# Hymba-style block in fp32 on one core: part of the depthwise convolution's taps as adding transfers, the layer norm dealt earlier

## Chip, core and metric

The kernel runs on one core of a Trainium2 chip. The metric is the device time of one execution in microseconds (us). The version before took 2039.97 us, the median of three runs (2035.58 to 2040.53).

## The reference, cut to what matters

The input x has 256 rows of 4096 columns, in float32. All weights are float32 and are read once from DRAM; w_in alone has 4096 x 14336 elements.

```python
xn = rms_norm(h, norm_in_g[i])
proj = xn @ w_in[i]
q, k, v, z_a, a_c, g_c, z_c = jnp.split(
    proj, np.cumsum([ATT_WIDTH] * 4 + [CONV_WIDTH] * 2)[:6].tolist(), axis=-1)
...
y_a = rms_norm(y_a, attn_out_g[i]) * jax.nn.silu(z_a)
y_c = conv_module(a_c, g_c, w_dw[i], b_dw[i], conv_ln_g[i], conv_ln_b[i], w_pw[i], b_pw[i])
y_c = rms_norm(y_c, conv_out_g[i]) * jax.nn.silu(z_c)
h = h + jnp.concatenate([y_a, y_c], axis=-1) @ w_out[i]
gate = jax.nn.sigmoid(rms_norm(h, ple_norm_g[i]) @ w_ple_gate[i] + b_ple_gate[i])
h = h + gate * (p[i] @ w_ple[i])
```

The change concerns conv_module: u = a * sigmoid(g), then for each of 2048 channels a causal filter of 31 taps over the 256 rows (u shifted by 30 - k rows, times w_dw[k], summed over k), plus a bias; then a layer norm over the channels, silu, and the product with w_pw. y_a is chunked attention with 16 heads of 128 and a relative bias.

## The kernel before, in words

**Products.** A product of 256 rows with 4096 x 1024 weights goes over 16 pairs of row blocks (`mixed_product`, one loop turn per pair, called a *step* here). A step loads two tiles of 512 KB with SyncE (SP) from a pool of five buffers. Each tile is split (`parts_of`): ScalarE casts it to float32r (`wh`, L218), VectorE subtracts that from the tile (`wl`, L219), and PE multiplies three times (high x high, low x high, high x low). A tile of a plain step thus costs 12 matmuls of 128x128 by 512 columns, and a plain step 24. A step called *seven* uses seven sums of blocks in place of eight products: 21 matmuls, with VectorE making the sums of weights (`ua`, `ub`, L442 to L447). There are three buffers each for wh and wl.

**The order of the products** is written out by hand: `glu_conv` 0 and 1 (columns of a and g), keys 0 (Q0 and K0), values (V0 and V1), then `attention(0)`, `glu_conv` 2 and 3, keys 1, `attention(1)`, keys 2, the layer norm's list, Q3/V2, `attention(2)`, K3/V3, `attention(3)`, then the product with w_pw, the gates z, w_out and w_ple_gate. Where a product ends, `scaled_pair` scales it by the row norm (L510), and `to_heads` transposes it (L851) and copies it (L856).

**Deferred work.** What has to be done between the steps is kept in the list `later`; after each step `deal` takes from it as many items as the product's `fills` say (`early_fills` for most products here), and one step of an attention from `heads`. Its instructions are issued behind the last cast, so the engines meet them in that place of their program. Between K3/V3 and w_pw the rest of the list is emptied in one go (`fill(len(later))`).

**The convolution.** `glu_conv(c)` makes u for 512 channels (four blocks of 128 channels, `uT`, channels on the partitions) and appends 4 x 31 taps to the list. A tap (`conv_tap`, L696) is one VectorE instruction on one block, `cv += uT shifted * w_dw[k]`, 226 to 256 columns wide. There are 16 blocks and so 16 x 30 such instructions, and 16 that start a sum.

**The layer norm** (`layer_norm_swish`) is a list too: sums over the blocks, mean by a matmul with a constant (`mean_w`), 16 centerings (L766), squares (L770) and their sums (L774), variance, then per block a multiplication and a silu on ScalarE (`swish`, L804), and a split into two float32r parts (`split`, ScalarE L814, VectorE L815), which is the stationary operand of w_pw. Empty items (`rest`) keep steps that wait for PE apart.

**Attention** (`attention(g)`, four heads) is five items in `heads`. The scores of two heads (L868, L869) get scale and bias on VectorE (L875) and their maximum (L879), ScalarE takes the exponential (L880); in the next item the weights are transposed and copied by VectorE (`pT`, L893), then multiplied by V. The bias comes by a transfer (`load_bias`), and one corner of it is overwritten by POOL (L939), which otherwise does almost nothing.

Of the kernel before, what the change touches and what calls it, by code (L numbers as in the profile page):

```python
# [21 lines left out]
NEG = -1e30  # L22
# [3 lines left out]
def hybrid_block(  # L26
# [157 lines left out]
    def behind_casts():  # L184
        return tc.issue_after(last_cast[0].ins) if last_cast else nullcontext()

    def fill(n):
        with behind_casts():
            for _ in range(min(n, len(later))):
                later.popleft()()  # L190

    heads = deque()
# [150 lines left out]
    def mixed_product(  # L343
# [67 lines left out]
        for n, (pair, seven) in enumerate(order):  # L411
            if n < done:
                continue
            if ahead:
                ahead(pair)
            wts = []
            for k in range(2):
                wt = wpool.tile([P, 2, NB], F32, tag="w", name="wt")
                nc.sync.dma_start(wt, two_columns(w, 2 * pair + k, col, apart))
                wts.append(wt)  # L420
            if n >= len(order) - n_left:
                for k in range(2):
                    tiles = left[2 * (n - len(order) + n_left) + k]
                    held.append((2 * pair + k, parts_of(wts[k], 2, tiles and tiles())[0]))
                deal(fills[n % len(fills)])
                continue
            if not seven:
                for k in range(2):
                    add_plain(n, k, *parts_of(wts[k], 2)[0])
                deal(fills[n % len(fills)])  # L430
                continue
            begins = not helper
            if begins:
                for name in ("P1", "P5", "P7", "P6"):
# [24 lines left out]
            add("P2", block(k1, 0), (w1h[:, 0], w1l[:, 0]), n, True)  # L459
            add("P3", s_of(3), (w1h[:, 1], w1l[:, 1]), n, True)  # L460
            add("P6", s_of(2), (ubh[:, 0], ubl[:, 0]), n, True)
            add("P4", block(k1, 1), (ubh[:, 1], ubl[:, 1]), n, True)
            if begins and on_begin:
                on_begin()
            if begins:
                tc.add_manual_dep(
                    made[first].ins, last_transpose[0].ins.name,
                    mybir.DependencyInfo(mybir.DependencyClass.NoSync, mybir.DependencyReason.DATA),
                    reason="transposes before the helpers take their banks",
                )  # L470
            if n == last_seven:
                on_helpers(helper)
            deal(fills[n % len(fills)])
        after.close()
        return (c, add_left) if left else c

# [210 lines left out]

    conv = []

    def conv_tap(cv, uT, i, b, k):  # L690
        if k == PAD:
            nc.vector.tensor_scalar(
                cv[:, i, :], uT[:, i, :], dw[:, b, k : k + 1], bdw[:, b : b + 1], ALU.mult, ALU.add
            )
        else:
            nc.vector.scalar_tensor_tensor(  # L696
                cv[:, i, PAD - k :], uT[:, i, : T + k - PAD], dw[:, b, k : k + 1],
                cv[:, i, PAD - k :], ALU.mult, ALU.add,
            )

    def glu_conv(c):
# [24 lines left out]
                uT[:, 2 * pair : 2 * pair + 2, :], pt.rearrange("q (i t) -> q i t", t=T)  # L726
            )
        cv = act.tile([P, 4, T], F32, tag="act", name="cv")
        for i in range(4):
            for k in reversed(range(TAPS)):  # L730
                later.append(partial(conv_tap, cv, uT, i, 4 * c + i, k))
        conv.append(cv)


    uS = []

    def layer_norm_swish():

# [76 lines left out]
            nc.vector.tensor_tensor(lo, conv[c][:, i, :], hi.bitcast(F32), ALU.subtract)  # L815

        n = len(conv)
        rest = [lambda: None] * 4
        later.extend(partial(total, c) for c in range(n))
        later.append(lambda: fold(st["s"]))  # L820
        later.extend(rest)
        later.append(lambda: mean(st["s"][:, 0, :]))
        later.extend(rest)
        for c in range(n):
            later.extend(partial(center, c, i) for i in range(4))
            later.append(partial(square, c))
        later.append(lambda: fold(st["q"]))
        later.extend(rest)
        later.append(lambda: variance(st["q"][:, 0, :]))
        later.extend(rest)  # L830
        later.append(lambda: diagonals(st["s"][:, 0, :]))
        later.extend(rest)
        later.append(lambda: spread(st["s"][:, 0, :]))
        later.extend(rest)
        for c in range(n):
            later.extend(partial(swish, c, i) for i in range(4))
        for c in range(n):
            later.extend(partial(split, c, i) for i in range(4))


    y_a = []
# [18 lines left out]

    def attention(g):
        qT, kT, v, bias = qs[g], ks.pop(g), vs.pop(g), biases.pop(g)
        y = qT.rearrange("q g (h d) -> q h g d", h=NH)
        held = {}

# [62 lines left out]
    def load_bias(g):  # L928
# [7 lines left out]
                ap=[[1, P], [span, GH], [1, T]],  # L936
            ),
        )
        nc.gpsimd.memset(bias[: P // 2, :, : P // 2], NEG)  # L939

    def queries(g, q):
        qs[g] = act.tile([P, GH, T], F32, tag="act", name="qT")
# [17 lines left out]
    def late_pool():  # L960
        nonlocal more
        first_sums.close()
        more = pool("more", 4)
        load_bias(3)

    n_g = H // GH
    assert n_g == CW // NB == 4
# [9 lines left out]
    keys(1, early_fills)  # L977
    attention(1)
    keys(2, early_fills)
    layer_norm_swish()  # L980
    load_bias(2)
    q, vs[2] = blocks((o_q + 3 * NB, o_v + 2 * NB), early, (4,))
    queries(3, q)
    attention(2)
    k, vs[3] = blocks(
        (o_k + 3 * NB, o_v + 3 * NB), valued, (5, 5, 4, 5, 4, 2, 3, 2, 3, 2, 3, 4, 4, 4, 4, 4),
        then=late_pool,
    )
    keyed(3, k)
# [8 lines left out]
        )  # L998
        return t

    fill(len(later))

    point = units("0 1 2 3 4 5 6 7")
    y_c = []
# [321 lines left out]
```

## Time and profile before

| what | before |
|---|---|
| median of three runs | 2039.97 us |
| the profiled execution | 2035.71 us |
| its span | 2033.9 us |
| PE busy | 2015.2 us, 99% |
| VectorE (DVE) busy | 1912.3 us, 94% |
| ScalarE (ACT) busy | 1184.6 us, 58% |
| GpSimd (POOL) busy | 7.7 us |
| moved by DMA | 412.28 MB, 203 GB/s on average |

The shares are of the span. A busy time counts overlapping instructions once; matmuls are pipelined, so a busy PE may still lose time between two starts. In rows of the timeline the first number is the start in us from the span's beginning, the second how long the group of instructions lasts; a bracket at the end holds the idle time of the engine ahead of it and what released it.

### The profile page before, as it was taken

What the parts mean: (1) busy time and instruction counts of PE and PEld (TensorE: products, weight loads), DVE (VectorE), ACT (ScalarE), POOL (GpSimd) and SP (SyncE); (2) the same over time, 40 slices, a digit from 0 to 9 for tenths busy, and PEclk for the clock granted to TensorE, in tenths of its full rate; (3) what the DMA queues carried; (4) which work ended last, traced back from release to release, by engine and by line L of the source; (5) the groups of instructions that cost most, each with busy time, mean ns of one, the idle gap of its engine ahead of it and who ended that gap; (6) DMA issues with size and microseconds to landing.
All of it is one profiled execution on the core that took longest, in us unless ns stands there. A gap on an engine that the chain in (4) does not pass through costs nothing.

```text
span 2033.9 us, 25980 instructions
## 1 busy us (share of the span) xinstructions
PE 2015.2 (99%) x9094; PEld 1661.5 (82%) x9094; DVE 1912.3 (94%) x2728; ACT 1184.6 (58%) x1530; POOL 7.7 (0%) x19
## 2 busy tenths in 40 slices
PE   9999999999999999999999999999999999999997
PEld 7888888888888888878888888888888888888876
DVE  7999999989999998986899999999999999999998
ACT  7655545555455544675566566676565666665555
POOL 0000000000000000000000000000000000000000
PEclk9999999999999999999999999999999999999999
DMA  8666666566665666555666666676666656666765
GB/s 288 194 196 203 202 196 197 176 196 192 205 205 166 196 199 195 175 186 186 190 217 202 197 210 210 220 232 206 208 199 212 209 187 207 199 223 204 234 208 179
DMA packets 157756, 412.28 MB, mean 203 GB/s; under 512 B 12974, under 2 KB 16190, under 8 KB 157626
## 3 DMA queue, kind: packets, MB, share of 16 engines
q1 hardware_dynamic: 156976, 409.80, 63.4%
q8 instruction: 71, 1.16, 0.2%
q10 hardware_dynamic: 650, 0.84, 0.1%
q14 instruction: 59, 0.48, 0.1%
HBM read 406.39 MB, written 4.19 MB: 202 GB/s over the span
## 4 chain that ended last, share of the span: by engine, by line
PE 53%; DVE 1%; issue 1%; ACT 0%; DMA 0%; POOLq 0%; POOL 0%; ACTq 0%; DVEq 0%
PE acc L386 40%; PE acc_P L386 12%; PE acc L233 1%; PE tmp_ps L170 1%; DVE wl L219 0%; DMA wt<-in_w_ple_dram 0%; DMA wt<-in_w_in_dram 0%; DVE big_t L815 0%; ACT wh L218 0%; ACT uh L218 0%; DVE ul L219 0%; ACT hc L1256 0%; DVE z L1196 0%; PE tmp_ps L891 0%; DVE z L1232 0%
## 5 line engine op out<-in xcount | busy, mean ns | idle before, releaser
L386 PE MATMUL acc<-wh,big_t 128*128 128x512 f32 x4252 | 1312.3, 391 | 0.8 <-DVE wh L577 0.5
L218 ACT CAST wh<-wt 128x1024 fp32r<-128x1024 f32 (+1 forms) x737 | 712.8, 978 | 562.0 <-PE acc L386 409.9
L386 PEld LDWEIGHTS acc<-wh,big_t 128*128 128x128 f32 x4252 | 795.4, 188 | 166.8 <-ACT big_t L156 1.3
L219 DVE TENSOR_TENSOR wl<-wt,wh 128x1024 fp32r<-128x1024 f32 (+1 forms) x737 | 823.6, 1130 | 49.8 <-ACT wh L218 46.7
L386 PE MATMUL acc<-wl,big_t 128*128 128x512 f32 x2126 | 819.7, 391 | 2.3 <-DVE wl L219 2.1
L386 PEld LDWEIGHTS acc<-wl,big_t 128*128 128x128 f32 x2126 | 398.8, 188 | 87.5 <-DVE wl L219 4.5
L696 DVE SCALAR_TENSOR_TENSOR cv<-uT,dw,cv 128x249 f32<-128x249 f32 (+22 forms) x480 | 209.4, 467 | 0.6
L218 ACT CAST uh<-ub 128x1024 fp32r<-128x1024 f32 x126 | 132.5, 1051 | 119.1 <-DVE ub L447 100.9
L218 ACT CAST uh<-ua 128x1024 fp32r<-128x1024 f32 x126 | 132.7, 1053 | 84.3 <-DVE ua L443 78.8
L386 PE MATMUL acc_P<-uh,big_t 128*128 128x512 f32 x528 | 161.9, 392 | 0.0
L219 DVE TENSOR_TENSOR ul<-ub,uh 128x1024 fp32r<-128x1024 f32 x126 | 153.9, 1221 | 7.3 <-ACT uh L218 6.7
L219 DVE TENSOR_TENSOR ul<-ua,uh 128x1024 fp32r<-128x1024 f32 x126 | 153.9, 1221 | 0.4 <-ACT uh L218 0.2
L386 PEld LDWEIGHTS acc_P<-uh,big_t 128*128 128x128 f32 x528 | 98.0, 188 | 23.0 <-ACT uh L218 3.5
L442 DVE TENSOR_TENSOR ua<-wt 128x512 f32<-128x512 f32 x126 | 86.7, 688 | 23.1 <-DMA wt<-in_w_in_dram 14.6
L386 PE MATMUL acc_P<-ul,big_t 128*128 128x512 f32 x264 | 101.6, 393 | 0.0
L443 DVE TENSOR_TENSOR ua<-wt 128x512 f32<-128x512 f32 x126 | 86.5, 686 | 1.9 <-DMA wt<-in_w_in_dram 1.8
L447 DVE TENSOR_TENSOR ub<-ub,wt 128x512 f32<-128x512 f32 x126 | 86.6, 687 | 0.6
L446 DVE TENSOR_TENSOR ub<-ua,wt 128x512 f32<-128x512 f32 x126 | 86.5, 687 | 0.3
L386 PE MATMUL acc_P<-wh,big_t 128*128 128x512 f32 x252 | 78.0, 390 | 0.0
L386 PE MATMUL acc<-uh,big_t 128*128 128x512 f32 x252 | 78.0, 390 | 0.0
L386 PE MATMUL acc_P<-uh,comb_t 128*128 128x512 f32 x228 | 70.3, 391 | 0.1
L386 PEld LDWEIGHTS acc_P<-ul,big_t 128*128 128x128 f32 x264 | 49.4, 188 | 13.1 <-DVE ul L219 2.8
(212 smaller groups left out, 1310.3 us busy)
## 6 DMA issues: line engine op xcount, KB each, us to landing
wt<-in_w_in_dram SPq DMA_DIRECT2D x447, 512.0 KB, 4.1
wt<-in_w_out_dram SPq DMA_DIRECT2D x128, 512.0 KB, 4.2
wt<-in_w_ple_gate_dram SPq DMA_DIRECT2D x128, 512.0 KB, 4.1
wt<-in_w_pw_dram SPq DMA_DIRECT2D x32, 512.0 KB, 4.7
hc<-in_x_dram SPq DMA_DIRECT2D x8, 512.0 KB, 5.8
wt<-in_w_ple_dram SPq DMA_DIRECT2D x8, 512.0 KB, 4.4
xin<-in_x_dram SPq DMA_DIRECT2D x7, 512.0 KB, 7.9
out_dram<-hc SPq DMA_DIRECT2D x12, 256.0 KB, 2.5
```

Source lines behind the costliest of these rows:

```text
L170: nc.tensor.transpose(pt[:, i * T + h * P : i * T + (h + 1) * P], src[:, h, b] if len(src.shape) == 4 else src[:, h, b * P : (b + 1) * P], ...
L218: nc.scalar.copy(wh[:, :kc, :], wt[:, :kc, :]),
L219: nc.vector.tensor_tensor(wl[:, :kc, :], wt[:, :kc, :], wh[:, :kc, :].bitcast(F32), ALU.subtract),
L233: nc.tensor.matmul(acc, a, b[:, k, :], start=kb == 0 and kind == 0, stop=kb == kblocks - 1 and kind == 2,)
L386: nc.tensor.matmul(banks[name], a, b, start=name not in begun, stop=final and ends[name] == n and kind == 2 and not (left and name in "P2 ...
L442: plus(ua[:, 0], w0[:, 0], w0[:, 1])
L443: plus(ua[:, 1], w0[:, 1], w1[:, 1])
L446: plus(ub[:, 0], ua[:, 0], w1[:, 1])
L447: plus(ub[:, 1], ub[:, 0], w1[:, 0])
L696: nc.vector.scalar_tensor_tensor(cv[:, i, PAD - k :], uT[:, i, : T + k - PAD], dw[:, b, k : k + 1], cv[:, i, PAD - k :], ALU.mult, ALU.add,)
```

## The change

Of the 31 taps of a convolution of four blocks, `ADDED[c]` (11, 9, 10 and 0 for c = 0 to 3, so 30 of 124 sums over four blocks) leave VectorE. For such a tap ScalarE writes `uT` shifted and scaled into a tile `tap` (two such tiles per convolution, from the pool `act`), pinned in program order; then a transfer issued by GpSimd adds the tile into `cv`, in two halves of two blocks (256 KB each). That makes 120 scalings on ScalarE and 60 transfers. They stand in a list of their own, `adds`, which gets a half's taps once the VectorE taps of that half are dealt; `add_half` issues one of them after two steps of three, while there are any.

In the list of deferred work, None now ends a `fill` (a border), and the empty items are gone. Q3/V2 is dealt by `early_fills` instead of four items a step, K3/V3 by other numbers, and the 16 splits are appended only when K3/V3 calls `late_pool`; the emptying before w_pw goes. The clearing of the bias corner moves from `load_bias` to `attention`, pinned.

```diff
+    adds = deque()
+
+    def add_half(n):
+
+        if adds and n % 3 < 2:
+            adds.popleft()()
+
     def fill(n):
+
         with behind_casts():
-            for _ in range(min(n, len(later))):
+            if n and later and later[0] is None:
+                later.popleft()
+            for _ in range(n):
+                if not later or later[0] is None:
+                    break
                 later.popleft()()
...
             deal(fills[n % len(fills)])
+            add_half(n)
...
+    ADDED = (11, 9, 10, 0)
+
+    def added_taps(cv, uT, c):
+
+        held = []
+
+        def tap(k, half):
+            blocks = slice(2 * half, 2 * half + 2)
+            if k < 2 and not half:
+                held.append(act.tile([P, 4, T], F32, tag="act", name="tap"))
+                nc.gpsimd.memset(held[k][:, :, :PAD], 0.0)
+            t = held[k % 2]
+            for i in range(blocks.start, blocks.stop):
+                b = 4 * c + i
+                pin(
+                    nc.scalar.activation(
+                        t[:, i, PAD - k :], uT[:, i, : T + k - PAD], AF.Identity,
+                        scale=dw[:, b, k : k + 1],
+                    )
+                )
+            nc.gpsimd.dma_start(cv[:, blocks], t[:, blocks], accum_op=ALU.add)
+
+        return [[partial(tap, k, half) for k in range(ADDED[c])] for half in range(2)]
...
-        for i in range(4):
-            for k in reversed(range(TAPS)):
-                later.append(partial(conv_tap, cv, uT, i, 4 * c + i, k))
+        halves = added_taps(cv, uT, c)
+        for half in range(2):
+            for i in (2 * half, 2 * half + 1):
+                for k in reversed(range(ADDED[c], TAPS)):
+                    later.append(partial(conv_tap, cv, uT, i, 4 * c + i, k))
+            if halves[half]:
+                later.append(partial(adds.extend, halves[half]))
...
-        later.append(lambda: fold(st["s"]))
-        later.extend(rest)
-        later.append(lambda: mean(st["s"][:, 0, :]))
-        later.extend(rest)
+        later.extend((lambda: fold(st["s"]), None, lambda: mean(st["s"][:, 0, :]), None))
...
-            later.extend(partial(split, c, i) for i in range(4))
+            splits.extend(partial(split, c, i) for i in range(4))
...
+        pin(nc.gpsimd.memset(bias[: P // 2, :, : P // 2], NEG))
...
-        nc.gpsimd.memset(bias[: P // 2, :, : P // 2], NEG)
...
         more = pool("more", 4)
         load_bias(3)
+        assert not later
+        later.extend(splits)
...
-    q, vs[2] = blocks((o_q + 3 * NB, o_v + 2 * NB), early, (4,))
+    q, vs[2] = blocks((o_q + 3 * NB, o_v + 2 * NB), early, early_fills)
     queries(3, q)
     attention(2)
     k, vs[3] = blocks(
-        (o_k + 3 * NB, o_v + 3 * NB), valued, (5, 5, 4, 5, 4, 2, 3, 2, 3, 2, 3, 4, 4, 4, 4, 4),
+        (o_k + 3 * NB, o_v + 3 * NB), valued, (3, 3, 3, 3, 3, 2, 3, 2, 3, 2, 3, 4, 4, 4, 4, 0),
         then=late_pool,
     )
...
-    fill(len(later))
+    assert not later
```

How the instructions move, at three places.

**VectorE (DVE) at the start of K3/V3**, before: the wl of the product's fourth and fifth tile (wl_7126, wl_7188) stand ahead of the first two heads' scores of attention 2 (s_7084, s_7096); cv_1028 is a convolution sum being centered.

```order
L219 TENSOR_TENSOR wl_7126<-wt_7107,wh_7125 128x1024
L219 TENSOR_TENSOR wl_7188<-wt_7183,wh_7187 128x1024
L875 SCALAR_TENSOR_TENSOR s_7084<-tmp_ps_7081,bias_6316 128x128
L875 SCALAR_TENSOR_TENSOR s_7084<-tmp_ps_7081,bias_6316 128x256
L879 TENSOR_REDUCE nm_7085<-s_7084 128x1 x2
L875 SCALAR_TENSOR_TENSOR s_7096<-tmp_ps_7093,bias_6316 128x128
L875 SCALAR_TENSOR_TENSOR s_7096<-tmp_ps_7093,bias_6316 128x256
L879 TENSOR_REDUCE nm_7097<-s_7096 128x1 x2
L766 TENSOR_TENSOR cv_1028<-cv_1028,mu_7079 128x256 x4
```

After: s_7284 and s_7296 are the scores of the next two heads, wl_7326 is the wl of the sixth tile and wl_7378 that of the seventh, pT_7364 and pT_7371 are transposed attention weights, ua_7481 is a sum of weights of a later step.

```order
L908 SCALAR_TENSOR_TENSOR s_7284<-tmp_ps_7281,bias_6426 128x256
L912 TENSOR_REDUCE nm_7285<-s_7284 128x1 x2
L908 SCALAR_TENSOR_TENSOR s_7296<-tmp_ps_7293,bias_6426 128x128
L908 SCALAR_TENSOR_TENSOR s_7296<-tmp_ps_7293,bias_6426 128x256
L912 TENSOR_REDUCE nm_7297<-s_7296 128x1 x2
L231 TENSOR_TENSOR wl_7326<-wt_7307,wh_7325 128x1024
L921 RECIPROCAL den_7286<-den_7286 128x2
L921 RECIPROCAL den_7298<-den_7298 128x2
L455 TENSOR_TENSOR ua_7481<-wt_7473 128x512
L926 COPY pT_7364<-tmp_ps_7360 128x384
L926 COPY pT_7371<-tmp_ps_7367 128x384
L231 TENSOR_TENSOR wl_7378<-wt_7373,wh_7377 128x1024
```

Before, the wl of the first five tiles stand ahead of the first scores and the sixth between the two blocks of scores. After, the fourth (wl_7246) stands directly behind the first block (rows ahead of these), the sixth behind the second block, and the seventh behind the copies of the transposed weights.

**ScalarE (ACT) at the same place**, before: casts of tiles (wh), the mean of the layer norm (mu_7079), the four exponentials of the first two heads (s_7084, s_7096), and the square of a convolution sum (sq_7219).

```order
L218 CAST wh_7125<-wt_7107 128x1024
L218 CAST wh_7187<-wt_7183 128x1024
L749 ACTIVATE mu_7079<-tmp_ps_7077 128x256
L880 ACTIVATE s_7084,den_7086<-s_7084,nm_7085 128x128
L880 ACTIVATE s_7084,den_7086<-s_7084,nm_7085 128x256
L880 ACTIVATE s_7096,den_7098<-s_7096,nm_7097 128x128
L880 ACTIVATE s_7096,den_7098<-s_7096,nm_7097 128x256
L218 CAST wh_7203<-wt_7185 128x1024
L770 ACTIVATE sq_7219<-cv_1028 128x1024
```

After: rs_7135 is the spread of the inverse deviation, the L846 rows are the silus on the convolution sums (cv), and ACT_TABLE_LOAD loads a function table.

```order
L230 CAST wh_7229<-wt_7225 128x1024
L791 ACTIVATE rs_7135<-tmp_ps_7132 128x256
L846 ACT_TABLE_LOAD
L846 ACTIVATE cv_1028<-cv_1028,prm_125 128x256 x3
L230 CAST wh_7245<-wt_7227 128x1024
L846 ACTIVATE cv_1028<-cv_1028,prm_125 128x256
L846 ACTIVATE cv_1765<-cv_1765,prm_125 128x256 x2
L913 ACT_TABLE_LOAD
L913 ACTIVATE s_7204,den_7206<-s_7204,nm_7205 128x128
```

Silus and table loads now stand between the casts and the exponentials of attention 2.

**PE at the start of the product with w_pw**, before: L851 transposes the last product for the heads, L868 and L869 are scores of attention 3, L386 is the product with w_pw.

```order
L386 MATMUL acc_7040<-wl,big_t 128x512
L851 MATMUL tmp_ps<-ident,z 128x128 x8
L868 MATMUL tmp_ps<-kT,qT 128x128
L869 MATMUL tmp_ps<-kT,qT 128x256
L386 MATMUL acc_7921<-wh,big_t 128x512 x2
L386 MATMUL acc_7923<-wh,big_t 128x512 x2
```

After (L883 transposes, L398 is the product, whose first step has 24 matmuls):

```order
L398 MATMUL acc_7158<-wl,big_t 128x512
L883 MATMUL tmp_ps<-ident,z 128x128 x8
L398 MATMUL acc_7993<-wh,big_t 128x512 x2
L398 MATMUL acc_7993<-wl,big_t 128x512
L398 MATMUL acc_7995<-wh,big_t 128x512 x2
L398 MATMUL acc_7995<-wl,big_t 128x512
```

And the end of that first step, still after, with the scores (L901, L902):

```order
L398 MATMUL acc_7994<-wl,big_t 128x512
L398 MATMUL acc_7996<-wh,big_t 128x512 x2
L398 MATMUL acc_7996<-wl,big_t 128x512
L901 MATMUL tmp_ps<-kT,qT 128x128
L902 MATMUL tmp_ps<-kT,qT 128x256
```

The scores, which stood directly behind the transposes, now stand behind the product's first step (24 matmuls); the wl matmuls are back beside their wh matmuls.

More of the change, by code (lines that the diff above doesn't have):

```diff
@@ L473, in mixed_product @@
             deal(fills[n % len(fills)])
+            add_half(n)
         after.close()
@@ L728, in glu_conv @@
         cv = act.tile([P, 4, T], F32, tag="act", name="cv")
-        for i in range(4):
-            for k in reversed(range(TAPS)):
-                later.append(partial(conv_tap, cv, uT, i, 4 * c + i, k))
+        halves = added_taps(cv, uT, c)
[5 more added lines that the diff above has]
+                later.append(partial(adds.extend, halves[half]))
         conv.append(cv)
-    uS = []
+    uS, splits = [], []
     def layer_norm_swish():
@@ L817, in layer_norm_swish @@
         n = len(conv)
-        rest = [lambda: None] * 4
         later.extend(partial(total, c) for c in range(n))
-        later.append(lambda: fold(st["s"]))
-        later.extend(rest)
-        later.append(lambda: mean(st["s"][:, 0, :]))
-        later.extend(rest)
+        later.extend((lambda: fold(st["s"]), None, lambda: mean(st["s"][:, 0, :]), None))
         for c in range(n):
@@ L826, in layer_norm_swish @@
             later.append(partial(square, c))
[L827 to L834, printed above, removed]
+        later.extend((lambda: fold(st["q"]), None, lambda: variance(st["q"][:, 0, :]), None))
+        later.extend((lambda: diagonals(st["s"][:, 0, :]), None, lambda: spread(st["s"][:, 0, :]), None))
         for c in range(n):
@@ L979, in hybrid_block @@
     keys(2, early_fills)
+    assert not adds
     layer_norm_swish()
     load_bias(2)
-    q, vs[2] = blocks((o_q + 3 * NB, o_v + 2 * NB), early, (4,))
+    q, vs[2] = blocks((o_q + 3 * NB, o_v + 2 * NB), early, early_fills)
     queries(3, q)
```

## The prediction

> **What bounds the kernel now.** I read the clock, the page's busy shares, the windows cut at the stages, the chain, and then the waits of PE.
>
> ```profile
> core 0: 2033.9 us, clock 0.998
> PE 2015.2 (99%) x9094; PEld 1661.5 (82%) x9094; DVE 1912.3 (94%) x2728; ACT 1184.6 (58%) x1530; POOL 7.7 (0%) x19
> ...
> 100.00:790.00 690.00, 689.20 (x3115) 569.84 (x3114) 678.45 (x1074) 362.13 (x432) 0.92 (x3) 1.00 0.63 195
> ...
> 1003.38 6.12 PE acc L386 x27
> ```
>
> The clock is granted in full. Columns of the windows are length, then PE, PEld, DVE, ACT, POOL, clock, DMA share and GB/s. From 100 to 790 us, where all convolution taps lie, VectorE is busy for 678 of 690 us, and PE for 689. Two engines at 98% and more: which one sets the pace? A busy PE says little, since matmuls overlap; its step from start to start says more. The chain gives 27 matmuls in 6.12 us, 0.227 us each, in a stage where PE waits for nothing. At that step the 3115 matmuls of the tap stretch would take 706 us, more than the 690 that it lasts (some are 128 columns wide and shorter), so there is no room for gaps. PE sets the pace there too; VectorE merely keeps up.
>
> ```profile
> PE acc L386 <- DVE wl L219: 2.1, 1, 2.1
> PE tmp_ps L125 <- DVE ssq_f L1134: 1.2, 1, 1.2
> PE tmp_ps L868 <- DVE kT L856: 0.8, 1, 0.8
> PE acc L386 <- DVE wh L577: 0.5, 1, 0.5
> PE acc_P L386 <- DVE ul L219: 0.3, 1, 0.3
> PE tmp_ps L851 <- DVE z L510: 0.3, 1, 0.3
> ```
>
> These are nearly all the waits of PE for another engine in the whole run. The 1.2 and the 0.5 lie at the end and the start, which the change leaves alone. That leaves 2.1 + 0.8 + 0.3 + 0.3 = 3.5 us that the change can win. The Trainium skill (Perfetto Trace Analysis, Identifying the Most-Contended Engine) would judge PE by LDWEIGHTS, 82% here, and VectorE by occupancy, 94%, and so work on VectorE first; it appears below as a rival.
>
> **The change, part by part.** It removes no matmul. *Taps.*
>
> ```profile
> L696 DVE SCALAR_TENSOR_TENSOR cv<-uT,dw,cv 128x249 f32<-128x249 f32 (+22 forms) x480 | 209.4, 467 | 0.6
> L156 ACT ACTIVATE big_t<-tmp_ps,prm 128x256 fp32r<-128x256 f32 x64 | 27.7, 470 | 4.1 <-DVE big_t L157 2.5 <-PE tmp_ps L170 1.6
> L904 ACT ACTIVATE qT<-tmp_ps,den 128x128 f32<-128x128 f32 x32 | 9.5, 362 | 0.1
> ```
>
> 30 taps of four blocks are 120 of the 480 instructions. 209.4/480 = 0.436 us each, so VectorE loses 52 us of work. ScalarE gains 120 scalings of 226 to 236 columns, between the rows of 128 and 256 columns, about 0.45 us and 54 us in all, against 328 us that it idles in the stretch. For PE both are worth only what waits now: the two waits of 0.3 us.
>
> *The transfers.* The trace has no adding transfer and none issued by POOL.
>
> ```profile
> q1 hardware_dynamic: 66026, 133.70, 62.9%
> ...
> DMA to landing us min/median/max: 3.3/4.4/5.7
> ...
> DMA to landing us min/median/max: 2.0/2.5/3.1
> ...
> 61.75 1.01 POOL L139 TENSOR_TENSOR r_x<-r_x,mhalf 128x2 f32<-128x2 f32 x1 [60.30 <-DVE r_x L138]
> 195.48 0.30 POOL L939 MEMSET bias<- 64x256 f32 x1 [132.73 <-DMA bias<-in_rel_table_dram]
> ```
>
> In the tap stretch 133.7 MB take 62.9% of 690 us, so 256 KB (0.262 MB) take 0.85 us of all DMA engines, and 1.7 if the target is read too: 60 of them are 51 to 102 us, a share of 0.70 to 0.78. The weights still fit. From issue to landing the nearest rows are rows of 256 KB, 4.4 us beside the weight stream (5.7 at most), and the stores at the end, 2.5 us with idle engines. I take 5.5 us: 4.4, and 1 for the issue on POOL by its longest row. Beyond 5.7 nothing in the trace excludes more. By the Trainium skill (DMA: Bandwidth & Descriptors, Anatomy of one DMA) a transfer issued by GpSimd takes 2.0 us plus its bytes at 436 GB/s, 2.6 us as an estimate; the sum below would not change.
>
> Who waits? Each add waits on POOL for the one before into the same half; ScalarE's scaling of tap k waits until the add of tap k-2 has read its tile, and behind it stand the casts that feed PE. Tap k comes three steps after tap k-2, and a step of 24 matmuls is 5.4 us (21 matmuls, 4.8), so some 15 us later: 5.5 us is covered. A product of 16 steps lasts 690/8 = 86 us and takes 11 adds, one in 7.8 us; only a landing beyond that builds a queue. The clearing of the bias corner (L939, 0.3 us) moves behind the adds on POOL, and VectorE's scores wait for it. It is covered while the last add ahead is issued a step before the scores; if not, it costs a landing, 4.4 us, for two of the four attentions. Price of the transfers: 0, from 0 to 2 × 4.4.
>
> *The end of the list.* Before, the last 20 items come in a burst between K3/V3 and the product with w_pw.
>
> ```profile
> 891.29 5.00 ACT L814 CAST big_t<-cv 128x256 fp32r<-128x256 f32 x16
> 893.07 2.71 DVE L510 SCALAR_TENSOR_TENSOR z<-acc,r_x,z 128x512 f32<-128x512 f32 x4
> 895.71 1.27 DVE L856 COPY kT<-tmp_ps 128x512 f32<-128x512 f32 x2
> 896.44 0.49 PE L868 MATMUL tmp_ps<-kT,qT 128*128 128x128 f32 x2 [0.82 <-DVE kT L856]
> 896.90 4.09 DVE L815 TENSOR_TENSOR big_t<-cv,big_t 128x256 fp32r<-128x256 f32 x12
> 902.19 1.20 PE L386 MATMUL acc<-wl,big_t 128*128 128x512 f32 x4 [2.13 <-DVE wl L219]
> ```
>
> Twelve splits (4.09 us) stand ahead of the first wl of w_pw: PE waits 2.13 us. Ahead of that, the scores wait 0.82 us for kT. In the changed order the splits are dealt inside K3/V3, and 24 matmuls of w_pw (5.4 us) stand between the transposes and the scores: z and kT, 2.71 + 1.27 = 3.98 us, are covered. Won: 2.13 + 0.82 = 2.95, with the two of 0.3, 3.5 us. It can't be more than about 4.5, since after these PE has no wait.
>
> *What moves up is now late elsewhere.* The silu steps land in the first five steps of K3/V3, between the exponentials of attention 2.
>
> ```profile
> L880 ACT ACT_TABLE_LOAD x3 | 3.8, 1283 | 0.1
> L804 ACT ACTIVATE cv<-cv,prm 128x256 f32<-128x256 f32 x16 | 8.2, 592 | 0.0
> ...
> 807.85 1.23 DVE L219 TENSOR_TENSOR wl<-wt,wh 128x1024 fp32r<-128x1024 f32 x1 [1.48 <-ACT wh L218]
> 809.00 0.62 DVE L875 SCALAR_TENSOR_TENSOR s<-tmp_ps,bias 128x128 f32<-128x128 f32 x2
> 811.10 1.42 DVE L766 TENSOR_TENSOR cv<-cv,mu 128x256 f32<-128x256 f32 x4
> 814.54 1.02 DVE L893 COPY pT<-tmp_ps 128x384 f32<-128x384 f32 x2
> 815.79 0.81 PE L386 MATMUL acc<-wh,big_t 128*128 128x512 f32 x2
> ```
>
> Counted out, the wl made at 807.85 is that of the product's fifth tile, which PE starts at 815.79: a lead of 6.7 us. In the new order ScalarE has 16 silus (8.2 us) and five table loads (1.28 each, 6.4) more there, less the four squares of the layer norm, and VectorE makes the fourth and fifth wl behind the scores: two tiles, 5.4 us, of lead are gone, and little is left. At three places I follow the order. The wl of the fourth and the sixth tile stand behind a score block: from the scores on, 2.1 us of VectorE (809.00 to 811.10), then 1.23; PE gets there after one tile and two matmuls, 2.72 + 0.45 = 3.17. Short by 0.2, and by 0.4 with a hand-over: 0.8 for both. The wl of the seventh tile stands behind the pT copies, which wait for transposes directly ahead of that tile on PE: 1.02 + 1.23 - 0.45 = 1.8 us late. Together 2.6, from 0 (VectorE is ahead after all) to 6 (each of them a whole hand-over of 2 us late).
>
> In Q3/V2 the sums of the layer norm move up as well.
>
> ```profile
> L484 DVE TENSOR_TENSOR z<-acc_P,z 128x512 f32<-128x512 f32 x9 | 6.2, 687 | 0.0
> L774 DVE TENSOR_TENSOR sq<-sq 128x1024 f32<-128x1024 f32 x3 | 3.7, 1221 | 0.0
> ```
>
> By the order, fifteen centerings, four sums of z and two sums of squares now stand between two wl there: 15 × 0.36 (a quarter of the 1.42 at 811.10) + 4 × 0.69 + 2 × 1.22 = 10.6 us, and 1.2 for the wl. The mean is ready some 8 to 9 us ahead of the tile (a step and a half), and the order puts eight wh matmuls (1.8 us) first: 11.8 against 9.8 to 10.8, less what neighbours on VectorE overlap. Late by 0 to 2.0; I take 0.7.
>
> **Sum.** -3.5 + 0 + 2.6 + 0.7 = -0.2 us. The profiled execution took 2035.71 us, 1.8 beside its span; the median of the three runs is 2039.97, and they lie 5 us apart. A change of -0.2 gives 2035.5 on the profiled level and 2039.8 on the median's. I forecast 2039.8: no change within 0.3% (6.1 us), about what a measurement of this kernel can tell.
>
> **The rivals.**
> - *Clean gain.* The lead at K3/V3 holds and nothing new is late: -3.5 to -4.5, or 2036. For it: ScalarE idles half the time there. Against: the wl behind the pT copies. 0.14, half of it shown as faster because the runs spread.
> - *VectorE is the bound.* By the skill's rule named above, the freed work shortens the tap stretch by its 52 us: 1988. Its 98% in the windows speaks for it, the step of PE against it. 0.02.
> - *Adds that land too slowly (slower).* From 7.8 us on, the scalings wait on ScalarE for the adds, and the casts behind them. At 9 us, twice the row of 256 KB, each of the 60 adds lags 1.2: 72 us less the head start of 15, some 2097. For it: the target is read and written, and POOL's issue is unseen. Against: 4.4 in the row, and a free third of DMA time. 0.11.
> - *The crowd in K3/V3 (slower).* Every hand-over there costs 2 us (6) and the centerings 2.0, with one landing of 4.4 at a bias corner: +12.4 - 3.5, so 2049. 0.07.
> - *The relief isn't one.* If each issue on POOL holds up VectorE for POOL's 0.30 to 1.01 us, 60 of them give back 18 to 61 of the 52 us. PE still covers it: 2040. 0.06. The Trainium skill (SBUF — State Buffer, Who interferes with whom) has such a lock between VectorE instructions with two inputs in SBUF and GpSimd ones that read it; no run here shows it.
>
> **How the numbers follow.** The forecast has 0.60: 0.51 inside 0.3%, 0.04 below, 0.05 above. Faster is 0.04 + 0.07 + 0.02 = 0.13; same 0.51 + 0.07 + 0.06 = 0.64; slower 0.05 + 0.11 + 0.07 = 0.23. The range starts at 2031, the lower run (2035.58) less 4.5, and ends at 2050, just past the crowd; it leaves out VectorE as the bound and the slow adds.
>
> **What would show it.** Right: PE without waits of 0.8 and 2.1 us at w_pw's start, new ones of 0.5 to 2 us on wl in the first 25 us of K3/V3, VectorE some 52 us less busy, the tap stretch as long as before. Adds landing in under 7.8 us, ScalarE never waiting for one. Wrong: PE's step in the tap stretch shrinking, or casts waiting on a scaling.

## Result, and the profile after

The changed kernel takes 2052.94 us, the median of four runs (2048.96 to 2054.73), against 2037.84 us (2035.58 to 2040.53) of the kernel before: a ratio of 1.0072, 95% interval 1.006 to 1.0084. It is slower by some 15 us. The forecast was 2039.8 within 2031 to 2050; the time lies above that range, and on the side that had 0.23.

First the clock and the busy shares of the profiled execution (2054.73 us), then two stages in the same columns as before, then what PE waits for between 100 and 790 us, where all convolution taps lie.

```profile
core 0: 2052.9 us, clock 0.996
```

```profile
PE 2022.6 (99%) x9094; PEld 1662.5 (81%) x9094; DVE 1872.9 (91%) x2608; ACT 1232.0 (60%) x1654; POOL 61.0 (3%) x85
```

```profile
100.00:790.00 690.00, 677.97 (x3040) 556.17 (x3039) 630.41 (x947) 396.48 (x544) 53.65 (x66) 1.00 0.74 212
...
1000.00:2000.00 1000.00, 999.07 (x4455) 822.34 (x4454) 957.56 (x1219) 610.98 (x759) 1.38 (x2) 1.00 0.65 209
```

```profile
PE acc L398 <- DVE wl L231: 4.6, 4, 1.8
PE tmp_ps L883 <- DVE z L524: 3.0, 4, 1.8
PE acc_P L398 <- DVE ul L231: 2.4, 2, 1.9
PE tmp_ps L933 <- DVE z L500: 1.2, 1, 1.2
PE tmp_ps L924 <- ACT s L913: 0.5, 3, 0.2
```

VectorE is busy for 39 us less in the whole run, and for 630 of 690 us in the tap stretch, where it was busy for 678. PE, which did 3115 matmuls there, does 3040: 75 fewer in the same time, 17 us at its step of 0.227 us. From 1000 us on hardly anything has changed. Instead of two waits of 0.3 us in the tap stretch PE has fourteen that add up to 11.7 us; VectorE's remainders (wl, ul) and its scalings of a product (z) are late, although VectorE is idle more often. So VectorE itself must be waiting. What for?

The 11.7 us are not all of the 17. After one of these waits, at 213.92 us, the trace shows PE at half the granted clock (the 0.50 in the row) for 3.4 us, which costs another 1.7 us. Before, the clock was whole from 7 to 2024 us.

```profile
214.80:218.20 3.40, 3.40 (x10) 2.62 (x9) 3.40 (x6) 1.65 (x2) 0.00 (x0) 0.50 0.99 287
```

VectorE's waits in the stretch are these:

```profile
DVE wl L231 <- ACT wh L230: 34.4, 28, 2.5
DVE ua L455 <- DMA wt<-in_w_in_dram: 15.9, 11, 2.6
...
DVE ua L456 <- DMA wt<-in_w_in_dram: 2.1, 3, 1.2
```

Before, VectorE waited for weight tiles (at ua) 1.8 us in this stretch, now 18.0. The tiles come later: the time from issue to landing of those issued between 160 and 690 us, before and then after.

```profile
DMA to landing us min/median/max: 3.4/4.1/5.7
```

```profile
DMA to landing us min/median/max: 3.5/4.7/8.2
```

The next rows show one wait for a tile, on VectorE and then on PE.

```profile
317.36 0.69 DVE L460 TENSOR_TENSOR ub<-ub,wt 128x512 f32<-128x512 f32 x1
317.96 0.98 DVE L734 SCALAR_TENSOR_TENSOR cv<-uT,dw,cv 128x247 f32<-128x247 f32 x2
321.16 0.69 DVE L455 TENSOR_TENSOR ua<-wt 128x512 f32<-128x512 f32 x1 [2.21 <-DMA wt<-in_w_in_dram]
321.77 1.22 DVE L231 TENSOR_TENSOR ul<-ub,uh 128x1024 fp32r<-128x1024 f32 x1
322.90 1.22 DVE L231 TENSOR_TENSOR wl<-wt,wh 128x1024 fp32r<-128x1024 f32 x1
```

```profile
324.18 0.50 PE L398 MATMUL acc<-wl,big_t 128*128 128x512 f32 x1 [1.76 <-DVE wl L231]
```

VectorE meets ua, the first sum of a later step's weights, and waits 2.21 us for that step's tile. Behind it stand ul and wl, which PE needs now; both are ready to be made, but VectorE works in order. PE then waits 1.76 us. In the trace, an adding transfer issued at 313.45 us landed at 320.02 (6.57 us); the weight tiles issued at 314.00 and 315.13 landed after 5.83 and 6.00 us, the latter at 321.13, just ahead of ua.

Not every wait of PE can be followed like this. Those at 495.19 us (1.86 us) and 634.67 us (1.75 us) stand behind 24 and 14 us in which VectorE works without a pause; that they too go back to a late tile is not shown by rows.

### The profile page after: what moved, and what is told of

It reads as the page before. It is cut to its first block, busy times and chain, and to the rows that moved or that the text cites. A ratio compares the mean times of both kernels' runs of the same rounds, so it can differ in the third digit from the quotient of the medians.

```text
span 2052.9 us, 26170 instructions
## 1 busy us (share of the span) xinstructions
PE 2022.6 (99%) x9094; PEld 1662.5 (81%) x9094; DVE 1872.9 (91%) x2608; ACT 1232.0 (60%) x1654; POOL 61.0 (3%) x85
## 4 chain that ended last, share of the span: by engine, by line
PE 59%; DVE 1%; issue 1%; ACT 0%; DMA 0%; POOLq 0%; POOL 0%; ACTq 0%; DVEq 0%
PE acc L398 44%; PE acc_P L398 12%; PE acc L245 1%; PE tmp_ps L170 1%; DVE wl L231 0%; DMA wt<-in_w_ple_dram 0%; DVE ul L231 0%; PE tmp_ps L902 0%; ACT uh L230 0%; PE tmp_ps L924 0%; ACT wh L230 0%; PE tmp_ps L934 0%; PE tmp_ps L935 0%; PE tmp_ps L933 0%; PE tmp_ps L901 0%
## 5 line engine op out<-in xcount | busy, mean ns | idle before, releaser
L398 PE MATMUL acc<-wh,big_t 128*128 128x512 f32 x4252 | 1313.5, 391 | 1.1 <-DVE wh L591 0.6
L398 PEld LDWEIGHTS acc<-wh,big_t 128*128 128x128 f32 x4252 | 796.1, 188 | 167.7 <-ACT big_t L156 1.4
L398 PE MATMUL acc<-wl,big_t 128*128 128x512 f32 x2126 | 819.9, 391 | 7.4 <-DVE wl L231 7.4
L398 PEld LDWEIGHTS acc<-wl,big_t 128*128 128x128 f32 x2126 | 399.0, 188 | 95.8 <-DVE wl L231 12.3
L398 PE MATMUL acc_P<-uh,big_t 128*128 128x512 f32 x528 | 161.7, 391 | 0.0
L734 DVE SCALAR_TENSOR_TENSOR cv<-uT,dw,cv 128x238 f32<-128x238 f32 (+22 forms) x360 | 157.5, 467 | 0.6
L398 PEld LDWEIGHTS acc_P<-uh,big_t 128*128 128x128 f32 x528 | 98.1, 188 | 22.8 <-ACT uh L230 3.2
L398 PE MATMUL acc_P<-ul,big_t 128*128 128x512 f32 x264 | 101.7, 393 | 1.0 <-DVE ul L231 1.0
L398 PE MATMUL acc<-uh,big_t 128*128 128x512 f32 x252 | 78.4, 392 | 0.0
L398 PE MATMUL acc_P<-wh,big_t 128*128 128x512 f32 x252 | 78.0, 390 | 0.0
L398 PE MATMUL acc_P<-uh,comb_t 128*128 128x512 f32 x228 | 70.6, 393 | 0.1
L724 POOL DMA_DIRECT2D cv<-tap x60 | 52.3, 872 | 570.1 <-ACT tap L719 386.4
```

The costliest lines, as they stand in the source:

```text
L398: nc.tensor.matmul(banks[name], a, b, start=name not in begun, stop=final and ends[name] == n and kind == 2 and not (left and name in "P2 ...
L724: nc.gpsimd.dma_start(cv[:, blocks], t[:, blocks], accum_op=ALU.add)
L734: nc.vector.scalar_tensor_tensor(cv[:, i, PAD - k :], uT[:, i, : T + k - PAD], dw[:, b, k : k + 1], cv[:, i, PAD - k :], ALU.mult, ALU.add,)
```

## The experiments

The theory (A): the adding transfers take DMA time from the weight stream, weight tiles land late, VectorE waits for them in order, and PE loses the time. Rivals: the scalings on ScalarE hold up the casts (B), or the order of the instructions itself loses it, whatever lands (C). Times are medians; the ratio is to runs of the kernel before on the same chip. A further column has the start of PE's 3200th matmul, at 707.0 us before, read from one trace each: it tells what has been lost up to the end of the tap stretch. The last column counts weight tiles issued between 160 and 690 us that took over 6 us to land.

| kernel | us | ratio to before, interval | 3200th matmul | tiles over 6 us |
|---|---|---|---|---|
| before | 2037.6 to 2038.4 | 1 | 0 | 0 of 168 |
| the change | 2052.94 | 1.0072 (1.006 to 1.0084) | +16.2 | 22 of 164 |
| no tap work | 2040.83 | 1.0009 (1.0 to 1.0018) | +0.6 | 0 of 168 |
| scalings only | 2042.99 | 1.0024 (1.0014 to 1.0034) | +5.4 | 3 of 167 |
| transfers only | 2046.41 | 1.0038 (1.0023 to 1.0053) | +13.7 | 29 of 165 |
| adds, old norm | 2065.08 | 1.0121 (1.0106 to 1.0137) | +27.3 | 13 of 159 |
| plain copies | 2048.11 | 1.0048 (1.0031 to 1.0065) | +8.8 | 5 of 165 |
| half the adds | 2044.17 | 1.0032 (1.0021 to 1.0044) | +3.8 | 13 of 167 |
| adds off the sevens | 2049.60 | 1.0061 (1.0046 to 1.0076) | +11.3 | 20 of 166 |
| fuller fills | 2041.10 | 1.0018 (1.0009 to 1.0028) | -0.4 | 0 of 168 |
| scalings, second unpinned | 2038.70 | 1.0004 (0.9995 to 1.0014) | +1.3 | 2 of 168 |
| adds, second unpinned | 2076.50 | 1.0191 (1.0177 to 1.0205) | +42.3 | 19 of 155 |
| splits in w_pw | 2032.61 | 0.9975 (0.9964 to 0.9986) | +0.1 | 1 of 168 |

**No tap work.**

```diff
-            for i in range(blocks.start, blocks.stop):
-                b = 4 * c + i
-                pin(
-                    nc.scalar.activation(
...
-            nc.gpsimd.dma_start(cv[:, blocks], t[:, blocks], accum_op=ALU.add)
```

> Leaves the 30 taps out altogether: neither scalings nor transfers, the rest of the changed order kept. Theory A (the adding transfers make the weight tiles land late, and PE loses the 16 us of the convolution stretch that way): weight tiles between 160 and 690 us land in 4.1 us on the median again and none over 6, VectorE's waits for a weight tile fall from 16 us to under 3, and the run takes some 2039, 14 below the changed kernel. Theory B (the scalings on ScalarE hold up the casts): also about 2039, with landings unchanged as a by-product. Theory C (neither; with fewer taps and another order VectorE meets its waits in a bad order, so the order itself loses the time): stays at 2050 or more.

Measured: 2040.83, ratio 1.0009; tiles land in 4.2 us on the median, none over 6. What is left of the change, its order and its layer norm, costs next to nothing, and C falls, but for one place that only the next kernel shows. VectorE's relief is worth nothing either: with its 52 us of taps gone and nothing put in their place, the time is that of before. VectorE still waits for tiles, 8.1 us at the first ua and 9.3 in all, not under 3, but none of these waits is over 1.7 us, and PE's start of its 3200th matmul is only 0.6 us late. So half of the 18.0 us that VectorE waits for tiles in the changed kernel come without any transfer, and such waits cost PE next to nothing.

```profile
DVE wl L231 <- ACT wh L230: 26.9, 26, 1.5
DVE ua L455 <- DMA wt<-in_w_in_dram: 8.1, 10, 1.6
```

**Scalings only.** The line with the transfer alone goes.

```diff
-            nc.gpsimd.dma_start(cv[:, blocks], t[:, blocks], accum_op=ALU.add)
```

> Keeps the 120 scalings on ScalarE and leaves the 60 transfers out, so the 30 taps don't reach the sum. Theory A: as the kernel without both, some 2040, VectorE's wait for casts (wl for wh) back from 34 us to about 10 between 100 and 790 us. Theory B: 2050 or more, the waits for casts stay above 25 us. Theory C: 2050.

Measured: 2042.99, 1.0024. Most of the loss goes with the transfers, but 3 us above no tap work stay, which neither A nor B had so. VectorE's wait for casts, which A expected at about 10 us, stays at 34.3; it is 26.9 in no tap work, where hardly anything is lost, so it was no sign of the loss. The 3 us lie in one place, on PE at 361 to 368 us:

```profile
361.09 0.81 PE L398 MATMUL acc<-wh,big_t 128*128 128x512 f32 x2
361.74 0.40 PE L398 MATMUL acc<-wl,big_t 128*128 128x512 f32 x1
362.30 0.33 PE L923 MATMUL tmp_ps<-ident,s 128*128 128x128 f32 x1 [0.16 <-ACT s L912]
362.79 0.88 PE L923 MATMUL tmp_ps<-ident,s 128*128 128x128 f32 x3 [0.17 <-ACT s L912]
...
367.55 0.49 PE L932 MATMUL tmp_ps<-z,pT 128*128 128x128 f32 x2 [1.20 <-DVE z L500]
```

These are attention 0's steps. Between its scores and the transposes of its weights (L923) stand three matmuls of the product; before, there were 24. PE arrives ahead of the exponentials, and soon after ahead of the values (z). From the matmuls ahead of this place to those behind it, PE's starts fall back by 3.9 us against before, here and in the changed kernel alike. It stands so in every kernel here that has all 30 taps' scalings pinned, the changed one among them (368 to 373 us there), and in none of the others.

**Transfers only.** Zeros are added, written once; the taps' values are missing.

```diff
-                nc.gpsimd.memset(held[k][:, :, :PAD], 0.0)
+                nc.gpsimd.memset(held[k], 0.0)
...
-                pin(
-                    nc.scalar.activation(
```

> Keeps the 60 transfers, but they add a tile of zeros that POOL writes once; the 120 scalings are left out, so the taps' values are missing. They may start earlier than in the changed kernel, since no scaling stands ahead of them. Theory A: about 2051, weight tiles land in 4.7 us on the median with some 20 over 6. Theory B: about 2039. Theory C: 2050 whatever lands.

Measured: 2046.41, and a wide spread (2043.78 to 2053.44); the profiled execution, 2053.44, has 29 tiles over 6 us, and its PE is 13.7 us late at the 3200th matmul with attention 0 in order. That execution is the slowest of six, so its counts are not those of the median. Against the kernel without tap work the transfers cost 0.3%, about 6 us. That has A's sign, but about half of its size (2051 was expected), and it is less than the 10 us by which the change exceeds scalings only; why is open, since the adds also start earlier here. As in the changed kernel the late tiles are among those in flight together with an add: 29 of 107 such tiles took over 6 us, and none of the 58 others (22 of 129 and none of 35 in the changed kernel).

```profile
DVE ua L455 <- DMA wt<-in_w_in_dram: 22.4, 15, 3.1
```

**Plain copies.**

```diff
-            nc.gpsimd.dma_start(cv[:, blocks], t[:, blocks], accum_op=ALU.add)
+            nc.gpsimd.dma_start(cv[:, blocks], t[:, blocks])
```

> The 60 transfers copy instead of adding (the same 256 KB into the same place, so the sums come out wrong); scalings, waits and order stay. Theory A1 (the adding transfers cost DMA time, 14.7% of it between 190 and 790 us for 14.68 MB, twice the share of a plain transfer by byte, and that time is what the weight tiles lose): the share halves to some 7.4%, weight tiles over 6 us fall from 22 to about 8, and the run takes about 2047, halfway between 2043 (scalings alone) and 2053. Theory A2 (it is the transfer as such, its issue on POOL or its place in the rings, not its bytes): stays at 2052.

The rows of the DMA queue issued by GpSimd (packets, MB, share of the 16 engines' time) and of the transfers' landing, between 190 and 790 us, of the changed kernel and then of this one:

```profile
q0 software_dynamic: 8064, 14.68, 14.7%
...
cv<-tap POOLq DMA_DIRECT2D x56, 256.0 KB, 5.1
```

```profile
q0 software_dynamic: 4480, 14.68, 6.5%
...
cv<-tap POOLq DMA_DIRECT2D x56, 256.0 KB, 4.3
```

For the same bytes an add takes 144 packets and 1.57 us of all engines (14.7% of 600 us over 56), a copy 80 packets and 0.70. With that, the tiles over 6 us fall from 22 to 5, and the time to 2048.11: above scalings only (1.0024) the transfers cost 0.24% in place of 0.48%. DMA time is halved, and so, by the medians, is the loss: that is A1, with an interval that overlaps the changed kernel's at the edge (up to 1.0065, and from 1.006). A2 had 2052. The number of the transfers and their place were the same in both, but not all else: POOL took 0.54 us to issue a copy and 0.86 for an add, and a copy lands sooner, so DMA time alone is not told apart from these.

**Half the adds.**

```diff
-        return [[partial(tap, k, half) for k in range(ADDED[c])] for half in range(2)]
+        return [[partial(tap, k, half) if k % 4 < 2 else lambda: None for k in range(ADDED[c])] for half in range(2)]
```

> Leaves out 13 of the 30 taps (scalings and transfers of them: 34 transfers stay), in the places where they stood. Theory A: the loss goes with the number of transfers: of the 13 us between this change and the kernel without the taps' work (2041 to 2053) some 57% stay, 2048, with about 12 weight tiles over 6 us. Rival: the loss hangs on a few places where an add meets a critical load, and then it may fall to 2043 or stay at 2052.

Measured: 2044.17, 1.0032, and 13 tiles over 6 us. That is below the 2048 of strict proportion: 34 transfers cost 0.23% above no tap work, where all 60 with their scalings cost 0.63%. The difference is attention 0, whose 24 matmuls stand in their place here: without its 3.9 us (0.19%) some 0.44% are left for 60 transfers, and 34 of them would cost 0.25%. So the loss does go with the number of transfers, as far as the interval tells.

**Adds off the sevens.**

```diff
-        if adds and n % 3 < 2:
+        if adds and (n < 3 or n > 8):
```

> All 60 adds, but dealt only behind the steps 0 to 2 and 9 to 15 of a product, so that none starts while the weight tiles of the seven-matmul steps (4, 6, 8, 10) are in flight; it does the whole computation. Theory A with the place (a late tile costs only where VectorE stands at the sum of weights ua and the casts' remainders wl and ul queue behind it): weight tiles still land late, 4.7 on the median, but VectorE's wait at ua falls from 16 us to under 6, and the run takes about 2045. Theory A without the place (any late tile costs): 2053.

Measured: 2049.60, 1.0061. VectorE's wait at ua falls only to 12.7 us, 20 tiles still take over 6 us, and the intervals of this ratio and the changed kernel's overlap. The expectation with the place fails, but the test is not a clean one. The edit does not keep the adds away from the tiles in question: of VectorE's 17 waits for tiles (14.0 us with both sums of ua), 8 waits with 6.0 us are for a tile that was in flight together with an add, where in the changed kernel it is 9 waits with 14.8 us. The other 8.0 us are about what no tap work has too (9.3). Whether the place of a late tile matters stays open.

**Adds, old norm.** The kernel before with scalings and transfers; each tap taken from the list leaves an empty item.

```diff
+            if ADDED[c]:
+                later.extend([lambda: None] * (ADDED[c] - 1))
+                later.append(partial(adds.extend, halves[i // 2]) if i % 2 else lambda: None)
```

> The kernel before with the transfers and scalings alone: the list of deferred work keeps its length (each tap that leaves it is replaced by an empty item), the layer norm, the splits and the fills stay as before. Theory A and B: before plus the loss of the convolution stretch, some 16 us: 2054, and PE still waits 2.1 us at the first step of w_pw. Theory C, if the layer norm's new place is what costs: 2040.

Measured: 2065.08, 1.0121, where 2054 was expected. PE still waits 2.1 us at the first step of w_pw, as expected. Fewer tiles are over 6 us than in the changed kernel (13 against 22), yet VectorE waits longer for tiles, 29.0 us against 18.0:

```profile
DVE ua L450 <- DMA wt<-in_w_in_dram: 24.6, 20, 2.7
DVE ua L451 <- DMA wt<-in_w_in_dram: 4.4, 7, 2.1
```

So the same transfers cost 10 us more in another arrangement of the remaining taps. The number of late tiles, then, does not tell the loss by itself. Which part of the arrangement does it was not tried further; it stays open. It says at least that the layer norm's new place did not cause the loss.

**Scalings and adds, the second convolution's scalings not pinned.** Two kernels, without and with the transfers.

```diff
-                pin(
+                (pin if c != 1 else lambda made: made)(
                     nc.scalar.activation(
```

> The same without the transfers (the 30 taps don't reach the sum). Theory D: as the kernel without scalings and transfers, 1.001 of before, some 2040, while the pinned scalings alone took 1.0024. Rival (ScalarE's load): 1.0024, 2043.

> The changed kernel with the scalings of the second convolution (9 taps) no longer pinned in program order; all of the computation is done. In the order of PE the 24 matmuls between attention 0's scores and the transposes of its weights are back, where the changed kernel has 3. Theory D (besides the transfers, the pinned scalings cost the 3 to 4 us that PE loses around 361 to 372 us, by that order): the waits there go and the run takes about 2049, 11 above before in place of 15. Rival: the scalings' load on ScalarE is what costs, wherever they stand: stays at 2053.

Without transfers: 2038.70, 1.0004, and attention 0's 24 matmuls are back. So the 3 us of the scalings were that order, not ScalarE's load: D holds for the scalings, and B falls. With the transfers the run takes 2076.50, far above the expected 2049. Here the second convolution's scalings follow each other closely on ScalarE, and now they wait for the adds:

```profile
ACT tap L719 <- DMA cv<-tap: 49.9, 16, 11.3
```

In the changed kernel that wait is 6.2 us in all. The adds land no later (5.1 us on the median, as in the changed kernel), but they come faster than they land, each waits for the one before, and the casts stand behind. After six of PE's waits the clock is halved for 3.4 us here, some 10 us of the loss. The pins that spoil attention 0 are also what spaces the adds.

**Fuller fills** and **splits in w_pw**: two ways to win the waits at w_pw without any transfer, from the kernel before.

```diff
-    q, vs[2] = blocks((o_q + 3 * NB, o_v + 2 * NB), early, (4,))
+    q, vs[2] = blocks((o_q + 3 * NB, o_v + 2 * NB), early, (5,))
...
-        (o_k + 3 * NB, o_v + 3 * NB), valued, (5, 5, 4, 5, 4, 2, 3, 2, 3, 2, 3, 4, 4, 4, 4, 4),
+        (o_k + 3 * NB, o_v + 3 * NB), valued, (5, 5, 4, 5, 4, 2, 3, 2, 3, 2, 3, 5, 5, 5, 5, 4),
```

> The kernel before, no transfers: Q3/V2 deals five items a step in place of four, K3/V3 five in four of its last five steps, so that the list is empty before w_pw without the change's other parts. If the gain at w_pw is real and the dearer Q3/V2 is covered by PE: PE's wait of 2.1 us at the first wl of w_pw goes, and the run takes 2 to 3 us less than before, 2036. If VectorE has no room for 16 items more in Q3/V2: new waits of PE there, 2039 or more.

```diff
-    fill(len(later))
+    fill(len(later) - 12)
...
-        acc = mixed_product(w_pw[0], c0 * NB, uS, None, point, None)
+        acc = mixed_product(w_pw[0], c0 * NB, uS, None, point, None, fills=(2, 2, 2, 2, 2, 2, 0, 0))
```

> The kernel before, no transfers and the layer norm where it was; of the 16 splits only the first four (those that w_pw's first two steps need) stay in the burst, the other 12 are dealt two a step behind w_pw's first six steps. If PE's wait of 2.1 us at w_pw's first wl is those 12 splits: it goes, nothing new comes, and the run takes about 2 us less than before, 0.999 of it. If something else is late there next: 1.000.

Fuller fills: 2041.10, 1.0018, slower. PE starts its 3600th matmul 1.9 us later than before and its 4000th 5.8 us: the work that left w_pw's start is late in Q3/V2 and K3/V3. Splits in w_pw: 2032.61, ratio 0.9975, faster than before and than the change, and the only one that is. It gains 5 us where 2 were expected. VectorE and PE at w_pw's start:

```profile
896.48 2.35 DVE L219 TENSOR_TENSOR wl<-wt,wh 128x1024 fp32r<-128x1024 f32 x2
898.75 0.75 DVE L815 TENSOR_TENSOR big_t<-cv,big_t 128x256 fp32r<-128x256 f32 x2
```

```profile
897.75 0.60 PE L869 MATMUL tmp_ps<-kT,qT 128*128 128x256 f32 x2
898.00 1.28 PE L386 MATMUL acc<-wl,big_t 128*128 128x512 f32 x4
```

The first wl now stand ahead of the remaining splits on VectorE, and the wl matmuls at 898.00 follow the scores with no wait. PE's order changed as well: eight wh matmuls now stand ahead of the scores, so the wait of 0.82 us for kT goes with that of 2.13. PE's 4400th matmul starts 4.1 us earlier than before, 3.7 of them won at this place.

## Why the prediction was wrong, point by point

- *PE bounds the tap stretch, not VectorE.* Right: VectorE without 52 us of taps left the time where it was (1.0009). The rival that VectorE is the bound is refuted; the rule of the Trainium skill (Perfetto Trace Analysis, Identifying the Most-Contended Engine) that points to VectorE first does not hold here.
- *The transfers cost nothing.* This is the step that failed: "The weights still fit", and the price of 0, from 0 to 8.8. The share of DMA time was right (1.57 us an add, forecast 0.85 to 1.7; 0.74 of the stretch, forecast 0.70 to 0.78), and so was the landing (3.3 to 8.1, median 5.1; forecast 5.5, from rows of which two were of 512 KB; one add of 60 took over 7.8). But the price was sought only with those who wait for an add, and ScalarE does wait little for them, 6.2 us. The price is paid by the other user of the same engines: the weight tiles, between 160 and 690 us 4.1 us on the median and never over 5.7 before, took up to 8.2. A free third of DMA time is an average; a tile in flight together with an add took 4.9 us on the mean, against 4.2 before, and the latest 2.5 us more than the latest before. VectorE then waits in order, and PE behind it. Between scalings only and the change that is 0.48%, some 10 us. That the transfers are the cause is shown by the kernels without them, with half of them and with copies; that it goes by way of late tiles is shown by rows for a part of PE's waits.
- *The rival of slow adds* had the sign but another mechanism: adds that land in over 7.8 us on the whole, and ScalarE stuck. That did not occur in the changed kernel. ScalarE did get stuck where the scalings were unpinned (49.9 us), though there the adds landed no later; they came closer together.
- *The scalings on ScalarE cost nothing.* Off by 3 to 4 us: attention 0's transposes stand behind 3 matmuls in place of 24. This was there to be read in PE's order, but the working looked at the order only from Q3/V2 on.
- *No relief from POOL's side.* The rival that POOL's issues hold up VectorE is not borne out: with 60 issues of 0.86 us, a wl took 1.220 us on the mean where it took 1.223 (both between 190 and 790 us). The lock in the Trainium skill (SBUF — State Buffer, Who interferes with whom) is one with GpSimd instructions that read SBUF; with these issues it does not show.
- *VectorE some 52 us less busy.* Its tap sums do take 52 us less (157.5 against 209.4), but its busy time fell by 39 only; why is open.
- *The end of the list.* The sum came out about right, by luck: its terms were not right. The waits of 2.13 and 0.82 us at w_pw are gone, as forecast, but not the two of 0.3 (0.25 and 0.63 even in no tap work). The centerings in Q3/V2, forecast late by 0.7 (0 to 2.0), were late by 2.5; the crowd in K3/V3, forecast 2.6, cost 0.4.

The burst of Q3/V2 on VectorE, its first row and its end, PE's wait behind it, and what PE waited for in K3/V3 (805 to 900 us):

```profile
789.69 3.44 DVE L808 TENSOR_TENSOR cv<-cv,mu 128x256 f32<-128x256 f32 x10
...
798.40 1.23 DVE L816 TENSOR_TENSOR sq<-sq 128x1024 f32<-128x1024 f32 x1
799.54 2.35 DVE L231 TENSOR_TENSOR wl<-wt,wh 128x1024 fp32r<-128x1024 f32 x2
```

```profile
800.82 1.20 PE L398 MATMUL acc<-wl,big_t 128*128 128x512 f32 x4 [2.50 <-DVE wl L231]
```

```profile
PE acc L398 <- DVE wl L231: 0.4, 1, 0.4
```

From 789.69 to 799.54 are 9.9 us, against 10.6 worked out. What was mis-sized is the lead: PE gets to the wl matmuls at 798.3, 8.6 us behind the start of the burst, where 9.8 to 10.8 were forecast. So the layer norm's part came to about -3.0 + 2.5 + 0.4, next to nothing, and in the kernel without tap work PE is 0.6 us late at its 3200th matmul and 0.8 at its 4400th. In the changed kernel's trace the wait of 2.5 us is followed by 3.4 us at half the clock, 1.7 us more, and PE goes from 16.2 to 18.1 us late. No tap work has the same wait of 2.50 us, and its clock stays whole.

## What to carry to other kernels

A free share of a queue's time says what fits, not when it lands: ask of each added transfer which load in flight beside it becomes late, and which engine meets that load in program order. Work taken from an engine that is busy but not the bound is worth nothing, so whatever pays for the relief is pure loss. And read the order of the bounding engine over the whole stretch that the change touches: three matmuls where 24 stood were visible before any run.

## What the runs showed of the hardware that was not expected

An adding transfer between tiles in SBUF took 2.2 times the DMA time of a plain one of the same 256 KB (1.57 against 0.70 us of all 16 engines) and 144 packets against 80, and landed after 5.1 us on the median against 4.3. By the fit in the Trainium skill (DMA: Bandwidth & Descriptors, Anatomy of one DMA) a transfer of this size issued by GpSimd takes 2.6 us, as an estimate; the fastest plain copy here took 2.2 and the median 4.3 beside the weight stream, the fastest add 3.3.

After some waits of PE the granted clock was 0.5 for 3.4 us, so that the wait cost 1.7 us more than its length: in the changed kernel after one of 1.84 and one of 2.50 us, in transfers only after one of 2.90 and one of 2.19. Other waits as long, one of 2.50 us in transfers only among them, were not followed by it; what decides is not shown.
